# Where the adaLN sums of a decoder layer are kept: two PSUM banks instead of SBUF

## The chip, the cores and the metric

The kernel runs on one core of a Trainium2 chip. The metric is the device time of one execution in microseconds. Besides DMA queues the core has five engines that each work through their own list of instructions in order: TensorE (PE: matmuls and transposes), VectorE (DVE), ScalarE (ACT), GpSimd (POOL) and SyncE (SP, which here issues most of the DMAs). SBUF is the large on-chip memory; PSUM is the small one, of eight banks of 128 partitions x 512 fp32 numbers, that matmuls write.

## The reference, cut to what matters

One decoder layer over 1024 rows of 1024 numbers, in fp32. A conditioning vector c gives six rows of 1024 (shift, scale and gate for each of two sub-layers):

```
cond = silu(c)
mod  = cond @ w_ada + b_ada                       # 1024 x 6144 matrix
sh1, sc1, gt1, sh2, sc2, gt2 = split(mod, 6)
h = rmsnorm(x) * (1 + sc1) + sh1
proj = h @ w_in                                   # q, k, v, indexer q/k/w, conv input
mixed = concat(sparse_attention(...), conformer_conv(...))
x = x + gt1 * (mixed @ w_out)
h = rmsnorm(x) * (1 + sc2) + sh2
x = x + gt2 * (relu(h @ w_up)**2 @ w_down)
out = rmsnorm(x)
```

The change concerns three of the six rows: gt1 (part 2 of the matrix's columns), sh2 (part 3) and sc2 (part 4).

## The kernel before, in words

Every fp32 product is made of three matmuls of rounded halves (hi x hi, hi x lo, lo x hi). So each weight tile, loaded from HBM as `wraw`, is split on the chip: ACT writes `whi` (L184), POOL writes `wlo` = wraw - whi (L185, 128x512). Four half tiles of wraw and six of whi and wlo go round.

The stages in order of time are: an opening (loads of x, first norm, sh1 and sc1, key/value projection), the projection of the indexer's queries (L137), the GLU input of the convolution (L126), the score chain (PE L616 and L617, ACT L618, DVE L621 and L623), a bit-by-bit search of the top-k threshold (ACT L704, DVE L706 and L707), beside it the convolution of 31 taps on DVE (L665 and L667), the attention, the output projection, and the MLP, which fills PE to the end.

A row of mod is not made by matmul alone. The eight 128-row slices of a part of w_ada (tile `wa`, 128x1024, 512 KB, two buffers) are loaded one after the other. DVE multiplies each by the slice's 128 numbers of cond, one a partition, and adds it to a sum of 128x1024, held as two halves of 512: `TENSOR_SCALAR` for the first slice (L547), `SCALAR_TENSOR_TENSOR` for the other seven (L545). A matmul with ones then sums over partitions. `ada_row` (L550 to L555) does that for gt1 by two matmuls of 128x512 (L554), one after the other through one PSUM bank (`po`), each emptied by DVE (L555). `ada_col` (L557 to L563) does it for sh2 and sc2 by eight matmuls of one column each half (L561), read by DVE (L563). Program order is part 2, `ada_row`, part 3, `ada_col`, part 4, `ada_col`.

In the opening sh1 and sc1 are made in the same way by `ada` (L357 to L366), but there the running sum lies in the PSUM bank `cv`, and only the last add writes to SBUF. The convolution (`conv_chunk`, L658 to L668) keeps its running sum in `cv` as well.

The PSUM tiles here are `mm` (two banks), `mc` (two), `tp` (two), `cv` (one) and `po` (one). A tile of a name with one bank can be written only when every reader of the tile before it, in program order, is done. `po` serves in turn the opening's sums over partitions, `ada_row`, `ada_col`, and then the attention's outputs (L772); `cv` serves the opening's `ada` and then the convolution's chunks.

Which instruction comes when on an engine is fixed at build time by a planner: every piece of work carries a number (`tc.cur_priority`, from the table PR), and among what its model of time holds to be ready the lowest number goes first. The evacuation of PSUM is at 30050, weight feed 32050, ada parts 130000 and up, key preparation (L481 to L499) 150500 and up, scores 200000 and up, GLU 205500, the first half's convolution 998450 (last of all). At run time the order stands: an instruction that waits holds back all behind it on its engine or queue, SP's DMA issues too.

Of the kernel before, what the change touches and what calls it, by code (L numbers as in the profile page):

```python
# [9 lines left out]
FT = mybir.dt.float32  # L10
# [5 lines left out]
OP = mybir.AluOpType  # L16
# [3 lines left out]
KD = D // 128  # L20
# [52 lines left out]
def layer(ctx, tc, x, c, positions, w_ada, b_ada, g_mix, w_in, conv_w, conv_b,  # L73
          conv_norm_g, conv_norm_b, w_out, g_mlp, w_up, w_down, g_final, out, dump=None):
    nc = tc.nc
    V, A, P, T, SP = nc.vector, nc.scalar, nc.gpsimd, nc.tensor, nc.sync
# [19 lines left out]
    psum = ctx.enter_context(tc.tile_pool(name="psum", bufs=1, space=bass.MemoryType.PSUM))  # L96
# [7 lines left out]
    def cv_tile(n=512):  # L104
        return psum.tile([128, n], FT, name="cv", bufs=1)
# [98 lines left out]
    cond = const.tile([128, 8], FT, name="cond")  # L204
# [34 lines left out]
    with tc.tile_pool(name="start", bufs=1, reuse_waits="tile") as st:  # L239
# [115 lines left out]
        accs = {}  # L355
# [180 lines left out]
    def ada_part(part):  # L536
        tc.cur_priority = PR["ada"] + 100 * part
        accs = [adacc[:, 2 * (part % 2) + s, :] for s in range(2)]
        for k in range(KD):
            wa = at.tile([128, D], FT, name="wa", tag="sb", bufs=2)  # L540
            SP.dma_start(wa, w_ada[k * 128:(k + 1) * 128, part * D:(part + 1) * D])
            for s in range(2):
                w = wa[:, s * 512:(s + 1) * 512]
                if k:
                    V.scalar_tensor_tensor(accs[s], w, cond[:, k:k + 1], accs[s], op0=OP.mult, op1=OP.add)  # L545
                else:
                    V.tensor_scalar(accs[s], w, cond[:, 0:1], None, op0=OP.mult)  # L547
        return accs

    def ada_row(part, dst, accs):  # L550
# [6 lines left out]
    def ada_col(part, dst):  # L557
        accs = ada_part(part)
        ps = psum.tile([128, 8], FT, name="po")
        for k in range(KD):  # L560
            T.matmul(ps[:, k:k + 1], accs[k // 4][:, (k % 4) * 128:(k % 4 + 1) * 128], ones[:, 0:1],  # L561
                     start=True, stop=True)
        V.tensor_tensor(dst, ps, bada[:, part * 8:part * 8 + 8], op=OP.add)  # L563

    sh2, a2 = modT[:, 16:24], modT[:, 24:32]
    gt1 = at.tile([128, D], FT, name="gt1")
    ada_row(2, gt1, ada_part(2))
    ada_col(3, sh2)
    ada_col(4, a2)
# [719 lines left out]
```

## Time and profile before

| | us |
|---|---|
| median of three runs | 1352.66 (1352.29 to 1352.8) |
| the profiled execution | 1357.23 |
| its span | 1355.5 |

| engine | busy us in the span | share | instructions |
|---|---|---|---|
| PE | 1251.4 | 92% | 6622 |
| DVE | 964.6 | 71% | 2068 |
| ACT | 692.6 | 51% | 1384 |
| POOL | 464.4 | 34% | 386 |

The times below are read from one profiled execution, counted from the start of its span. Its own time is the span and 1.7 us around it. "Busy" is time in which an instruction of the engine runs; a wait is idle time, and is put down to what ended it.

### The profile page before, as it was taken

To read this page: it belongs to the slowest core of one execution; us is meant where nothing else is said; L and a number is where in the kernel's file an instruction comes from. 1 tells how busy PE (TensorE), PEld (TensorE's weight loads), DVE (VectorE), ACT (ScalarE), POOL (GpSimd) and SP (SyncE) were. 2 spreads that over 40 slices of the span, in tenths; PEclk is the share of its full clock that TensorE was granted. 3 is DMA by queue.
4 is the path that set the end of the run, shared out by engine and by line. 5 is a ranking of instruction groups with operands and counts; after the bars stand their busy time and mean duration, and the time that the engine had idled before them with its cause. 6 is when DMAs were issued, how large, how long until landed. Compare 5 with 4: busy or idle time off the path is not lost.

```text
span 1355.5 us, 19285 instructions
## 1 busy us (share of the span) xinstructions
PE 1251.4 (92%) x6622; PEld 1050.2 (77%) x6622; DVE 964.6 (71%) x2068; ACT 692.6 (51%) x1384; POOL 464.4 (34%) x386
## 2 busy tenths in 40 slices
PE   2777899999998999989999999799999999999997
PEld 2676799878987788768887889678878877888875
DVE  6879798988898999988779871662443485444357
ACT  6533377666756988648996643333112232333332
POOL 1132434422144254432133127222212244444453
PEclk9888899999999999989999999899999999999999
DMA  9457634521223132221112122361111243323322
GB/s 314 148 171 231 181 98 129 140 71 56 86 87 125 47 101 87 80 73 59 47 55 71 55 94 90 124 208 54 47 39 47 62 143 121 104 91 101 93 94 93
DMA packets 135690, 139.55 MB, mean 103 GB/s; under 512 B 8877, under 2 KB 109833, under 8 KB 135592
## 3 DMA queue, kind: packets, MB, share of 16 engines
q1 hardware_dynamic: 135424, 138.22, 33.1%
q8 instruction: 52, 0.85, 0.3%
q14 instruction: 46, 0.38, 0.1%
q10 hardware_dynamic: 168, 0.11, 0.0%
HBM read 126.23 MB, written 12.06 MB: 102 GB/s over the span
## 4 chain that ended last, share of the span: by engine, by line
PE 66%; DVE 20%; DMA 4%; ACT 4%; issue 3%; POOL 1%; ACTq 0%; POOLq 0%; SPq 0%; DVEq 0%
PE mm L126 25%; PE mc L126 14%; PE tp L126 7%; PE mm L137 5%; DMA wa<-in_w_ada_dram 3%; DVE cv L667 2%; PE po L865 2%; PE tp L858 2%; DVE acc L545 1%; ACT sj L704 1%; PE po L772 1%; DVE acc L1042 1%; PE mc L846 1%; PE mc L847 1%; DVE e L682 1%
## 5 line engine op out<-in xcount | busy, mean ns | idle before, releaser
L185 POOL TENSOR_TENSOR wlo<-wraw,whi 128x512 fp32r<-128x512 f32 x310 | 413.1, 1341 | 773.3 <-ACT whi L184 682.1
L184 ACT ACTIVATE whi<-wraw 128x512 fp32r<-128x512 f32 x310 | 193.5, 629 | 297.9 <-PE mm L126 142.5
L126 PE MATMUL mm<-half,whi 128*128 128x512 f32 x608 | 204.8, 405 | 0.1
L667 DVE SCALAR_TENSOR_TENSOR cv<-glu,cwT,cv 128x512 f32<-128x512 f32 x232 | 174.0, 750 | 0.7
L704 ACT ACTIVATE sj<-score,bits 128x512 uint8<-128x512 f32 (+5 forms) x186 | 163.3, 878 | 17.1 <-DVE bits L707 8.3
L126 PE MATMUL mc<-half,whi 128*128 128x512 f32 x416 | 150.4, 393 | 0.5 <-ACT half L981 0.5
L126 PE MATMUL mm<-whi,uh 128*128 128x512 f32 x344 | 138.5, 403 | 7.1 <-DVE acc L1042 3.2
L126 PE MATMUL mm<-whi,ul 128*128 128x512 f32 x344 | 137.4, 399 | 3.3 <-DVE ul L1010 3.3
L126 PE MATMUL mm<-wlo,uh 128*128 128x512 f32 x344 | 136.8, 398 | 0.0
L1042 DVE TENSOR_TENSOR acc<-mm,acc 128x512 f32<-128x512 f32 x152 | 104.5, 688 | 44.4 <-PE mm L126 43.1
L1008 DVE TENSOR_TENSOR sq<-sq 128x512 f32<-128x512 f32 x42 | 46.0, 1096 | 126.2 <-ACT sq L1007 126.2
L126 PE MATMUL mc<-half,wlo 128*128 128x512 f32 x336 | 132.1, 393 | 0.0
L126 PEld LDWEIGHTS mm<-half,whi 128*128 128x128 f32 x608 | 115.3, 193 | 20.2 <-ACT half L981 0.3
L126 PE MATMUL mm<-half,wlo 128*128 128x512 f32 x304 | 124.4, 409 | 0.0
L137 PE MATMUL mm<-whi,half 128*128 128x256 f32 x640 | 120.1, 284 | 3.5 <-DVE wi L474 2.8
L137 PEld LDWEIGHTS mm<-whi,half 128*128 128x128 f32 x640 | 101.4, 191 | 5.5 <-issue 2.9
L126 PE MATMUL mc<-h,whi 128*128 128x512 f32 x256 | 100.2, 391 | 0.0
L126 PEld LDWEIGHTS mc<-half,whi 128*128 128x128 f32 x416 | 79.0, 190 | 17.3 <-ACT half L981 0.8
L137 PE MATMUL mm<-wlo,half 128*128 128x256 f32 x320 | 90.6, 283 | 0.4 <-POOL wlo L185 0.4
L126 PEld LDWEIGHTS mm<-whi,uh 128*128 128x128 f32 x344 | 65.3, 190 | 26.1 <-DVE acc L1042 6.5
L126 PEld LDWEIGHTS mm<-whi,ul 128*128 128x128 f32 x344 | 65.3, 190 | 18.1 <-DVE ul L1010 4.2
L126 PEld LDWEIGHTS mm<-wlo,uh 128*128 128x128 f32 x344 | 65.2, 190 | 13.0
(314 smaller groups left out, 2619.2 us busy)
## 6 DMA issues: line engine op xcount, KB each, us to landing
wraw<-in_w_up_dram SPq DMA_DIRECT2D x108, 256.0 KB, 2.8
wraw<-in_w_down_dram SPq DMA_DIRECT2D x108, 256.0 KB, 2.8
wa<-in_w_ada_dram SPq DMA_DIRECT2D x48, 512.0 KB, 4.9
wraw<-in_w_in_dram SPq DMA_DIRECT2D x33, 256.0 KB, 2.8
wraw<-in_w_in_dram SPq DMA_DIRECT2D x64, 128.0 KB, 3.0
wraw<-in_w_out_dram SPq DMA_DIRECT2D x32, 256.0 KB, 2.6
xs<-in_x_dram SPq DMA_DIRECT2D x8, 512.0 KB, 8.1
x<-in_x_dram SPq DMA_DIRECT2D x8, 512.0 KB, 5.1
```

The costliest lines, as they stand in the source:

```text
L126: T.matmul(ps, x, y, start=first and i == 0, stop=last and i == 3 * n - 1)
L137: T.matmul(ps[:, i * 256:(i + 1) * 256], rows[i][k][x], w[k][y], start=m == 0, stop=m == len(steps) - 1)
L184: A.activation(hi, raw, AF.Copy)
L185: P.tensor_tensor(lo, raw, hi.bitcast(FT), op=OP.subtract)
L545: V.scalar_tensor_tensor(accs[s], w, cond[:, k:k + 1], accs[s], op0=OP.mult, op1=OP.add)
L667: V.scalar_tensor_tensor(y if tap == CK - 1 else s, gl[:, tap:tap + 512], cwT[:, j, tap:tap + 1], s, op0=OP.mult, op1=OP.add)
L682: V.tensor_scalar(jk, score[b], thr, 0.0, op0=op, op1=OP.add, accum_out=dst[:, b:b + 1])
L704: A.activation(sj[:, :L], score[b], AF.Sign, bias=bits[:, col].bitcast(FT), accum_out=cnt[:, col])
L858: T.transpose(t[:, 2 * i + u, :], sbp[u][:, (i0 + i) * 128:(i0 + i + 1) * 128], ident)
L865: T.matmul(po[:, hp % 2], vhl[:, i0 + i, g].rearrange("p a d -> p (a d)"), p[:, 2 * i:2 * i + 2, :], start=i0 + i + j == 0, stop=i0 + i == ...
L1008: V.tensor_tensor(sq, sq, sq, op=OP.mult)
L1042: V.tensor_tensor(acc[b][:, cols], ps, acc[b][:, cols], op=OP.add)
```

## The change

In `ada_part`, which makes parts 2, 3 and 4, the running sum of the first half of the columns is kept in a `cv` tile and that of the second half in a new `po` tile. The multiplication of the first slice writes there, slices 1 to 6 read and write there, and slice 7 reads there and writes the finished sum into the SBUF tile `adacc`, from which the matmuls with ones read as before. The loads, the number and shapes of instructions, and the other parts (0 and 1 in the opening, 5 in the MLP) stay.

```diff
     def ada_part(part):
         tc.cur_priority = PR["ada"] + 100 * part
         accs = [adacc[:, 2 * (part % 2) + s, :] for s in range(2)]
+        sums = [cv_tile(), psum.tile([128, 512], FT, name="po")]
         for k in range(KD):
             wa = at.tile([128, D], FT, name="wa", tag="sb", bufs=2)
             SP.dma_start(wa, w_ada[k * 128:(k + 1) * 128, part * D:(part + 1) * D])
             for s in range(2):
                 w = wa[:, s * 512:(s + 1) * 512]
                 if k:
-                    V.scalar_tensor_tensor(accs[s], w, cond[:, k:k + 1], accs[s], op0=OP.mult, op1=OP.add)
+                    V.scalar_tensor_tensor(accs[s] if k == KD - 1 else sums[s], w, cond[:, k:k + 1], sums[s],
+                                           op0=OP.mult, op1=OP.add)
                 else:
-                    V.tensor_scalar(accs[s], w, cond[:, 0:1], None, op0=OP.mult)
+                    V.tensor_scalar(sums[s], w, cond[:, 0:1], None, op0=OP.mult)
         return accs
```

## Rows read from the trace of the kernel before

**Rows 1.** The profile's page: busy time, share of the span, instructions.
```profile
PE 1251.4 (92%) x6622; PEld 1050.2 (77%) x6622; DVE 964.6 (71%) x2068; ACT 692.6 (51%) x1384; POOL 464.4 (34%) x386
```

**Rows 2.** By stretch: busy us of PE, PEld, DVE, ACT, POOL; PEclk, DMA share, GB/s.
```profile
93.00:107.00 14.00, 13.02 (x106) 12.52 (x106) 13.69 (x33) 5.61 (x15) 8.45 (x6) 1.00 0.63 181
107.00:119.00 12.00, 4.43 (x17) 2.70 (x16) 11.11 (x35) 3.39 (x7) 1.27 (x1) 0.61 0.85 235
...
163.00:180.00 17.00, 17.00 (x66) 13.59 (x66) 14.05 (x26) 7.19 (x13) 5.81 (x7) 0.87 0.23 62
```

**Rows 3.** Who waited for whom, 55 to 170 us: total us, times, longest.
```profile
DVE acc L545 <- DMA wa<-in_w_ada_dram: 10.3, 7, 3.9
...
PE po L554 <- DVE gt L555: 7.6, 1, 7.6
```

**Rows 4.** DVE's groups by shape, 75 to 163 us: busy us, mean ns.
```profile
L545 DVE SCALAR_TENSOR_TENSOR acc<-wa,cond,acc 128x512 f32<-128x512 f32 x42 | 36.5, 907 | 10.5 <-DMA wa<-in_w_ada_dram 10.3
...
L547 DVE TENSOR_SCALAR acc<-wa,cond 128x512 f32<-128x512 f32 x6 | 2.6, 480 | 0.0
...
L667 DVE SCALAR_TENSOR_TENSOR cv<-glu,cwT,cv 128x512 f32<-128x512 f32 x2 | 1.5, 744 | 0.0
```

**Rows 5.** Instructions on tiles acc and cv: ns minimum/median/maximum, first and last start.
```profile
L545 DVE SCALAR_TENSOR_TENSOR acc<-wa,cond,acc x42: 739/747/1787, 76.8 to 157.3; 128x512 f32<-128x512 f32 x42
...
L667 DVE SCALAR_TENSOR_TENSOR cv<-glu,cwT,cv x232: 703/749/757, 146.9 to 552.1; 128x512 f32<-128x512 f32 x116
...
L366 DVE TENSOR_SCALAR cv<-wa,cond x4: 747/750/754, 19.2 to 50.4; 128x512 f32<-128x512 f32 x4
```

**Rows 6.** DVE in order of time: start, us, instruction, idle before.
```profile
101.20 2.45 DVE L545 SCALAR_TENSOR_TENSOR acc<-wa,cond,acc 128x512 f32<-128x512 f32 x2
103.57 1.26 DVE L484 TENSOR_TENSOR kk<-ra,rb 128x16 f32<-128x16 f32 x1
...
107.22 0.88 DVE L547 TENSOR_SCALAR acc<-wa,cond 128x512 f32<-128x512 f32 x2
...
110.17 0.18 DVE L481 TENSOR_TENSOR ra<-kk,cs 128x32 f32<-128x32 f32 x1
...
112.25 2.42 DVE L545 SCALAR_TENSOR_TENSOR acc<-wa,cond,acc 128x512 f32<-128x512 f32 x2
114.59 0.68 DVE L555 TENSOR_TENSOR gt<-po,gt 128x512 f32<-128x512 f32 x1
...
117.43 0.69 DVE L555 TENSOR_TENSOR gt<-po,gt 128x512 f32<-128x512 f32 x1 [0.64 <-PE po L554]
```

**Rows 7.** PE in order of time.
```profile
105.56 1.02 PE L554 MATMUL po<-acc,ones 128*128 128x512 f32 x2
...
115.32 2.08 PE L554 MATMUL po<-acc,ones 128*128 128x512 f32 x2 [7.57 <-DVE gt L555]
```

**Rows 8.** POOL in order of time.
```profile
101.49 3.31 POOL L185 TENSOR_TENSOR wlo<-wraw,whi 128x512 fp32r<-128x512 f32 x2 [2.32 <-ACT whi L184]
...
121.54 1.30 POOL L185 TENSOR_TENSOR wlo<-wraw,whi 128x512 fp32r<-128x512 f32 x1 [7.42 <-ACT whi L184]
```

**Rows 9.** SP's queue in order of time.
```profile
108.12 0.33 SPq L541 DMA_DIRECT2D wa<-in_w_ada_dram  x1
108.51 0.43 SPq L179 DMA_DIRECT2D wraw<-in_w_in_dram  x1
```

**Rows 10.** DVE in order of time, later.
```profile
133.42 0.87 DVE L547 TENSOR_SCALAR acc<-wa,cond 128x512 f32<-128x512 f32 x2
...
162.35 0.17 DVE L563 TENSOR_TENSOR modT<-po,vT 128x8 f32<-128x8 f32 x1 [3.80 <-PE po L561]
```

**Rows 11.** PE busy in the matmuls of L126 alone, by stretch.
```profile
107.00:121.50 14.50, 3.89 (x9) 0.65 0.86 251
121.50:126.40 4.90, 4.77 (x17) 1.00 0.68 200
```

**Rows 12.** Who PE waited for, 163 to 280 us.
```profile
PE tp L524 <- DVE qs L519: 4.4, 1, 4.4
```

## The prediction

> **What bounds the kernel now.** I read the page's busy times first, then the busy time by stretch around the changed lines, then who waited for whom, then the engines in order of time. PE is busy for 92% of the span [rows 1], so the 104 us in which it idles are what can be won, and an edit on DVE pays where DVE holds PE up. The changed additions lie between 76.8 and 157.3 us [rows 5]. The reader is to see in [rows 2] that one stretch there is poor: from 107 to 119 us PE works 4.43 of 12 us, at a mean clock of 0.61, while DVE works 11.11 of 12; before it PE works 13.02 of 14, and from 163 to 180 all 17. [rows 3] names the cause: one wait of 7.6 us of the second L554 matmul for the `po` bank, which DVE empties in L555. The first L554 ran at 105.56 [rows 7]; its L555 came only at 114.59 [rows 6], because DVE was late and had other work in front. So in this stretch PE is bound by DVE's order of instructions, and DVE in part by w_ada's loads (10.3 us in seven waits [rows 3]).
>
> **The additions that change place.** L545 takes 747 ns in the median but 1787 at most [rows 5], and 907 in the mean [rows 4]. The same instruction with its sum in PSUM (L667: one input in SBUF, one in `cv`) takes 749 in the median and 757 at most, in 232 cases [rows 5]. So PSUM as such gives nothing (747 against 749); what can go is the tail. Its cause shows at 101.20: a pair that takes 2.45 us, where two medians make 1.49, lies on POOL's wlo work of 101.49 to 104.80 [rows 6, 8]. If all 42 lose their tail, that is 42 x (907 - 747) = 6.7 us of DVE time. The last slice's six still write SBUF, but read one input there, as L667's do. POOL's work goes on, though, and DVE's key preparation between the additions has the same trouble: L484 at 103.57 takes 1.26 us beside the same POOL work, where L481, of twice the size, takes 0.18 without it [rows 6]. A delay that an addition no longer meets can hit the next small instruction. The bounds are therefore 0 (all passed on) and 6.7 us; I take 4.5, nearer to the upper, since POOL's instruction is partly over by the time the next small one comes.
>
> The Trainium skill, "SBUF — State Buffer", section "Who interferes with whom", says that a VectorE instruction with two SBUF inputs contends with a GpSimd instruction that reads SBUF, and one with at most one such input, outside the 2-port modes, doesn't. The rows of L667 agree with the second half. The same section counts two-input tensor_tensor instructions among those that contend, which is what speaks against this change: the key preparation stays exposed. Taken alone, that rule would put the passed-on share near all and the DVE gain near 0; the POOL row at 101.49, which covers both an addition and an L484, is why I don't go so far.
>
> **The first multiplications.** Six L547 take 480 ns from SBUF to SBUF [rows 4]; the same instruction into `cv` in the opening takes 750 [rows 5]. That costs 6 x 0.27 = 1.6 us of DVE. Net on DVE: 4.5 - 1.6 = 2.9 us saved, with bounds -1.6 and +5.1.
>
> **The bank `cv`.** It is free since the opening. But the convolution's first chunk, which now starts on it during part 4 (first tap at 146.9 [rows 5], two taps by 163 us [rows 4]), must wait until part 4 is done, near 157. That moves two taps and the first multiplication, some 3 x 0.75 = 2.2 us, behind 157. DVE then stands idle for 3.80 us until L563 at 162.35 [rows 10], so there is room. The cost is between 0 (all in that gap) and 2.2 us on DVE, if the planned order puts them behind L563; I take 0.5.
>
> **The bank `po`, and the order it enforces.** Now the second half's first multiplication of part 3 has to come behind both L555 of part 2. Today all of part 3's first two slices and the pair at 112.25 stand ahead of the first L555: from 107.22 (0.88 us) to 112.25 (2.42 us) three pairs, 0.88 + 1.41 (an estimate: two medians less their overlap) + 2.42 = 4.7 us [rows 6]. Of these only first-half instructions can stay in front, and with two buffers of `wa` at most two of them: 0.75 + 0.75 = 1.5. So DVE reaches the first L555 about 3.2 us earlier by order, and another 1 us earlier at least by the tail of the 101.20 pair: near 110.4 instead of 114.59. If the key preparation of later positions is moved up into the hole, half of the 3.2 may be lost. PE's wait of 7.6 us shrinks to some 3.4, with bounds 1 and 7.6. At the shortened wait I expect less of the clock loss too: after the present one the two matmuls take 2.08 us where the first pair took 1.02 [rows 7].
>
> In part 4 the same rule puts L547 behind L563 of part 3; L547 came at 133.42 [rows 10], which is already behind that L563 in DVE's order, so nothing moves. PE's L554 and L561 wait for the sums to leave `po`, which is the same last addition for which they wait already: no cost.
>
> **What is late next.** A slot of `wa` is released by both halves of a slice. Part 3's third slice is loaded at 108.12 [rows 9]; with the first slice's second half behind the second L555 (117.43 now, some 113 then) that load goes to about 114. SP issues in order, and 0.4 us behind it stands a load for w_in [rows 9]. If the planned order keeps that sequence, the GLU's weights are late by about 5 us. Is there room? The fourth weight tile of the chunk is split at 121.54 [rows 8]. By 121.5 PE had done 9 of the chunk's 48 L126 (8 row blocks x 3 products x 2 column groups in the code) and by 126.4 it had done 26 [rows 11]; the second half of the weights is first needed with the 25th, near 126. So PE could run some 4 to 5 us earlier before it met the weights as they come now; that caps the gain. The planner, whose model also sees the `wa` load waiting, may put the w_in load in front.
>
> **The sum.** PE wait 7.6 - 3.4 = 4.2 us, and with it up to 1 us of clock, capped by the weights at 4 to 5; I take 4. The DVE saving of 2.9 less 0.5 is partly the same gain (it makes the L555 early) and is not added. From 163 to 180 PE is full [rows 2], so work that starts earlier ends earlier; the search behind it is a chain from the last score, and PE waits again for DVE behind that search (4.4 us [rows 12]), so the shift goes through instead of being swallowed. Sum: 1357.23 - 4 = 1353.2 in terms of the profiled execution. That execution is 4.57 us (0.34%) above the median of the runs; I carry the difference over: 1352.66 - 4 = 1348.7.
>
> **Rivals.**
> 1. *The gain is swallowed.* DVE's delays are passed on to the key preparation (net -1.6 us on DVE), other ready work fills the hole in front of L555, and the chain of w_ada loads still sets the pace: 10.3 us in seven waits [rows 3] speak for it. Then PE's wait stays near 7, and the time stays within 1352.66 +- 2.7, say 1352. Against it: instructions that stood ahead of L555 can't stand there any more.
> 2. *The `po` bank makes it slower.* The planned order fills the hole with key preparation, so that L555 stays at 114.59 and 117.43. Then part 3's first slice ends only near 119, the load of 108.12 goes out some 10 us later, and the w_in load behind it on SP too. The tile split at 121.54 would come near 131.5, against a need near 126: PE waits 5.5 us there, and has won nothing at L555: 1352.66 + 5.5 = 1358.2. The point from which this decides is a second L555 later than about 113 + 2, with SP's order as it is. For it: SP's present order; against it: the planner places loads by when it thinks their slots come free.
> 3. *More is won.* The whole 7.6 us and the clock loss of 2 us go, and the earlier chain of w_ada loads brings the weights earlier by half of the 6.7 us: some 8 us, 1344.7. Against it stands the cap by the weights.
> 4. *A new planned order behind 163 us.* The planner sees new release times, and its choices further on (convolution against search and scores, all on DVE) can fall otherwise, by some microseconds either way; I price it at +- 3 us, an estimate from DVE waits of PE such as that of 4.4 us [rows 12], and hold it in the width of the cases.
>
> **How the numbers follow.** A change of this kernel can be told from none from about 0.2%, 2.7 us. Forecast (1345.5 to 1350): 0.40. Swallowed: 0.27. Slower through the bank or a worse order: 0.26. More won: 0.07. So faster 0.47, same 0.27, slower 0.26. The range of 8 in 10 leaves out the far ends on both sides: 1343.5 to 1358; the likeliest case's own is 1345.5 to 1350.
>
> **What would show it.** Right: L545's longest falls to about 0.76 us while L481 to L499 keep cases above 1 us; the L547 take 0.75; the wait of PE at L554 falls to 2 to 5 us and the stretch of 107 to 119 us shows more than 6 us of PE at a higher clock; the score chain and the search start some 4 us earlier. Wrong: PE's wait at L554 stays at 7 us or turns into one for weights (POOL's wlo or a w_in load) before 135 us; the convolution's first chunk holds PE at the convolution's transposes; or the shift is there at 180 us and gone by 480 us, because a search or a score chain was ordered worse.

## The result and the profile after

The changed kernel takes 1366.24 us in the median of four runs (1364.97 to 1367.66), the kernel before 1352.73 (1352.29 to 1355.49): a ratio of 1.0096, 95% interval [1.0074, 1.0117]. It is slower by 1%. I had forecast 1348.7 us, faster by 0.3%; the result lies outside the range as well. The profiled execution took 1367.66 us, its span 1365.9. In what follows the changed kernel's lines stand one or two higher than before: L546 are the additions (L545 before), L549 the first multiplications (L547), L556 and L557 the gate's matmul and its evacuation (L554, L555), and from there on two are added.

The page's busy times of the changed kernel, which answer to [rows 1]:

```profile
PE 1253.1 (92%) x6622; PEld 1051.1 (77%) x6622; DVE 970.4 (71%) x2068; ACT 696.2 (51%) x1384; POOL 462.4 (34%) x386
```

The number of instructions is the same. PE is busy 1.7 us longer and idle 8.7 us longer in a span that is 10.4 us longer. First the stage that was changed. By tile, in the changed kernel (minimum, median and maximum ns, first and last start), as in [rows 5]:

```profile
L546 DVE SCALAR_TENSOR_TENSOR cv<-wa,cond,cv x18: 744/755/756, 76.6 to 162.7; 128x512 f32<-128x512 f32 x18
L549 DVE TENSOR_SCALAR cv<-wa,cond x3: 744/747/751, 75.1 to 142.9; 128x512 f32<-128x512 f32 x3
L546 DVE SCALAR_TENSOR_TENSOR acc<-wa,cond,cv x3: 733/735/747, 101.3 to 165.6; 128x512 f32<-128x512 f32 x3
L546 DVE SCALAR_TENSOR_TENSOR po<-wa,cond,po x18: 743/750/752, 77.3 to 163.4; 128x512 f32<-128x512 f32 x18
```

The additions' tail, 1787 ns at most before, is gone: none takes over 0.76 us. The multiplications cost 0.75 as foretold. DVE in order of time in the changed kernel shows where the tail went, as in [rows 6]:

```profile
95.46 1.28 DVE L498 CAST nh<-kk 128x256 fp32r<-128x256 f32 x1
...
109.23 1.25 DVE L484 TENSOR_TENSOR kk<-ra,rb 128x16 f32<-128x16 f32 x1
110.51 1.21 DVE L481 TENSOR_TENSOR ra<-kk,cs 128x32 f32<-128x32 f32 x1
111.64 1.30 DVE L481 TENSOR_TENSOR rb<-kk,sn 128x32 f32<-128x32 f32 x1
112.97 1.17 DVE L483 TENSOR_TENSOR kk<-ra,rb 128x16 f32<-128x16 f32 x1
114.07 0.17 DVE L484 TENSOR_TENSOR kk<-ra,rb 128x16 f32<-128x16 f32 x1
114.15 0.68 DVE L557 TENSOR_TENSOR gt<-po,gt 128x512 f32<-128x512 f32 x1
...
117.00 0.69 DVE L557 TENSOR_TENSOR gt<-po,gt 128x512 f32<-128x512 f32 x1 [1.09 <-PE po L556]
...
117.93 0.75 DVE L549 TENSOR_SCALAR po<-wa,cond 128x512 f32<-128x512 f32 x1
```

POOL in the same stretch, in the kernel before and then in the changed one:

```profile
112.84 1.27 POOL L185 TENSOR_TENSOR wlo<-wraw,whi 128x512 fp32r<-128x512 f32 x1 [8.04 <-ACT whi L184]
```

```profile
109.18 4.93 POOL L185 TENSOR_TENSOR wlo<-wraw,whi 128x512 fp32r<-128x512 f32 x4 [3.75 <-ACT whi L184]
```

Key preparation filled the room in front of the first L557 because it took over the delays: beside POOL's run of 109.18 to 114.11 four small instructions need 1.17 to 1.30 us each, where the next one, as POOL ends, needs 0.17. Key preparation itself is hardly more than before: between part 2's last addition and this evacuation stand 31 small instructions of key preparation (on the tiles kk, ra and rb) where 27 stood, about 0.7 us more. But POOL, which split one weight tile there, now splits four in a row, and that makes some 4.2 us (an estimate: 4.93 us for four that need 0.7 undelayed). So L557 came at 114.15 where it was 114.59 before; without these delays it would have come near 110. The first L556 ran 1.5 us earlier than in [rows 7], and PE's wait for `po` grew from 7.57 to 8.95. PE in order of time, then who DVE waited for from 55 to 170 us, as in [rows 3]:

```profile
104.05 1.02 PE L556 MATMUL po<-acc,ones 128*128 128x512 f32 x2
114.88 2.07 PE L556 MATMUL po<-acc,ones 128*128 128x512 f32 x2 [8.95 <-DVE gt L557]
```

```profile
DVE cv L546 <- DMA wa<-in_w_ada_dram: 16.4, 10, 5.1
```

And DVE waits 16.4 us for `wa` where it waited 10.3. The second half's first multiplication of part 3 stands at 117.93, behind the second L557; until then its slice's buffer is held and no new slice can be loaded. SP's queue of the changed kernel:

```profile
102.75 0.33 SPq L542 DMA_DIRECT2D wa<-in_w_ada_dram  x1
103.12 3.52 SPq L179 DMA_DIRECT2D wraw<-in_w_in_dram  x7
110.47 2.10 SPq L179 DMA_DIRECT2D wraw<-in_w_in_dram  x4
118.71 1.32 SPq L542 DMA_DIRECT2D wa<-in_w_ada_dram  x2
```

For 16 us no slice is loaded (the load of 108.12 [rows 9] is that of 118.71). The loads for w_in stand ahead of it now, and PE waits for weights nowhere from 104 to 180 us. Part 4's last addition starts at 166.22 instead of 157.3.

Yet the time isn't lost at once. Same events before and after, each row first of the kernel before, then of the changed kernel (rows by tile; first and last start at the end of each): the search's first sign count, the last evacuation of the attention's scores, the last evacuation of a gate.

```profile
L704 ACT ACTIVATE sj<-score,bits x186: 599/888/1164, 180.6 to 724.0; 128x512 uint8<-128x512 f32 x31, 128x384 uint8<-128x384 f32 x31, 128x1024 uint8<-128x1024 f32 x31, 128x896 uint8<-128x896 f32 x31
...
L848 DVE CUSTOM_DVE_ANT_0 sb<-mc,score x32: 673/688/692, 615.7 to 785.9; 128x512 f32<-128x512 f32 x32
...
L555 DVE TENSOR_TENSOR gt<-po,gt x4: 678/692/693, 114.6 to 994.5; 128x512 f32<-128x512 f32 x4
```

```profile
L706 ACT ACTIVATE sj<-score,bits x186: 600/878/1155, 174.8 to 730.6; 128x512 uint8<-128x512 f32 x31, 128x384 uint8<-128x384 f32 x31, 128x1024 uint8<-128x1024 f32 x31, 128x896 uint8<-128x896 f32 x31
...
L850 DVE CUSTOM_DVE_ANT_0 sb<-mc,score x32: 669/692/693, 619.8 to 801.0; 128x512 f32<-128x512 f32 x32
...
L557 DVE TENSOR_TENSOR gt<-po,gt x4: 679/692/693, 114.2 to 1006.9; 128x512 f32<-128x512 f32 x4
```

The search starts 5.8 us earlier, as forecast or better. At 800 us the kernel is 15.1 us late, at 1000 us 12.4, at the end 10.4 (the spans). What lies between shows by stretch (PE busy and its instructions first, then the other engines; granted clock, DMA share and GB/s last), before and after:

```profile
270.00:430.00 160.00, 152.95 (x1044) 136.54 (x1044) 142.91 (x306) 100.50 (x226) 48.74 (x47) 0.99 0.26 81
...
440.00:460.00 20.00, 19.78 (x93) 15.48 (x94) 18.51 (x44) 19.19 (x36) 3.57 (x3) 0.90 0.09 26
460.00:480.00 20.00, 18.64 (x80) 13.88 (x79) 18.84 (x48) 19.05 (x39) 7.12 (x6) 1.00 0.25 79
```

```profile
270.00:430.00 160.00, 152.96 (x1011) 134.15 (x1010) 143.29 (x297) 97.72 (x218) 45.21 (x43) 0.99 0.23 74
...
440.00:460.00 20.00, 18.16 (x78) 14.24 (x78) 17.42 (x44) 17.51 (x32) 1.91 (x2) 0.74 0.18 55
460.00:480.00 20.00, 15.06 (x60) 10.67 (x59) 19.40 (x52) 19.32 (x41) 5.83 (x5) 0.85 0.22 67
```

From 270 to 430 us the same busy time holds 33 instructions fewer. From 440 to 480 PE idles 6.8 us instead of 1.6, at 0.74 and 0.85 of its clock. At the middle of that place PE, in order of time, before and after:

```profile
465.24 0.39 PE L126 MATMUL mm<-whi,uh 128*128 128x512 f32 x1
```

```profile
475.68 0.79 PE L618 MATMUL mc<-keys,qT 128*128 128x512 f32 x1 [1.91 <-DVE score L625]
...
477.38 0.79 PE L126 MATMUL mm<-whi,uh 128*128 128x512 f32 x1 [0.15 <-ACT uh L1006]
477.97 0.63 PE L126 MATMUL mm<-wlo,uh 128*128 128x512 f32 x1
```

PE's first down product of the MLP starts 12 us later. In PE's order score products (L618) now stand in front of it; they wait for buffers that DVE empties (L625) between ten taps of the convolution, and behind the waits the clock is at the lower of its levels (1.2 GHz: granted 0.50 from 476 to 482 us; the matmuls of 512 columns take 0.63 us, 0.39 before). None of these instructions touches the sums that the change moved. Either the change's local delay (its banks) comes out so late, or the planner, which plans all instructions anew when one dependence changes, has drawn a worse order.

### The profile page after: what moved, and what is told of

It is laid out like the page before. It is cut to its first block, busy times and chain, and to the rows that moved or that the text cites. A ratio compares the mean times of both kernels' runs of the same rounds, so it can differ in the third digit from the quotient of the medians.

```text
span 1365.9 us, 19296 instructions
## 1 busy us (share of the span) xinstructions
PE 1253.1 (92%) x6622; PEld 1051.1 (77%) x6622; DVE 970.4 (71%) x2068; ACT 696.2 (51%) x1384; POOL 462.4 (34%) x386
## 4 chain that ended last, share of the span: by engine, by line
PE 59%; DVE 11%; ACT 2%; issue 2%; POOL 1%; DMA 1%; POOLq 0%; DVEq 0%; ACTq 0%; SPq 0%
PE mm L126 24%; PE mc L126 14%; PE tp L126 7%; PE mm L137 4%; PE po L867 2%; PE tp L860 2%; PE mc L848 1%; PE mc L849 1%; DVE acc L1044 1%; DVE g2acc L1196 1%; DMA wa<-in_w_ada_dram 1%; DVE e L684 1%; PE mc L618 1%; DVE score L625 1%; PE po L774 1%
## 5 line engine op out<-in xcount | busy, mean ns | idle before, releaser
L126 PE MATMUL mm<-half,whi 128*128 128x512 f32 x608 | 205.6, 405 | 1.0 <-ACT half L983 0.6
L126 PE MATMUL mc<-half,whi 128*128 128x512 f32 x416 | 149.0, 390 | 0.5 <-ACT half L983 0.5
L126 PE MATMUL mm<-whi,uh 128*128 128x512 f32 x344 | 139.8, 407 | 3.3 <-DVE acc L1044 1.8
L126 PE MATMUL mm<-whi,ul 128*128 128x512 f32 x344 | 138.3, 402 | 2.2 <-DVE ul L1012 2.2
L126 PE MATMUL mm<-wlo,uh 128*128 128x512 f32 x344 | 138.6, 403 | 0.0
L126 PEld LDWEIGHTS mm<-half,whi 128*128 128x128 f32 x608 | 115.0, 192 | 21.6 <-DVE acc L1044 1.1
L126 PE MATMUL mc<-half,wlo 128*128 128x512 f32 x336 | 131.1, 390 | 0.0
L126 PE MATMUL mm<-half,wlo 128*128 128x512 f32 x304 | 122.7, 403 | 0.0
L126 PE MATMUL mc<-h,whi 128*128 128x512 f32 x256 | 99.9, 390 | 0.0
L126 PEld LDWEIGHTS mc<-half,whi 128*128 128x128 f32 x416 | 78.0, 188 | 17.0 <-ACT half L983 0.8
L126 PEld LDWEIGHTS mm<-whi,uh 128*128 128x128 f32 x344 | 66.2, 192 | 21.1 <-DVE acc L1044 4.4
L126 PEld LDWEIGHTS mm<-whi,ul 128*128 128x128 f32 x344 | 66.0, 192 | 17.7 <-DVE ul L1012 3.3
L126 PEld LDWEIGHTS mm<-wlo,uh 128*128 128x128 f32 x344 | 66.3, 193 | 13.6
```

The source lines that it names most:

```text
L126: T.matmul(ps, x, y, start=first and i == 0, stop=last and i == 3 * n - 1)
```

## The experiments

Three theories. **A**: the bank `cv` is the loss, since the convolution starts behind part 4. **B**: the bank `po` is, since part 3 waits for the gate. **C**: the loss is the new planned order as such. Where the expectations speak of D, that is A and B together: what the change itself does.

**One part of the change at a time.** In `ada_part`, one edit for each kernel:

```diff
 e1   sums = [cv_tile(), accs[1]]
 e2   sums = [accs[0], psum.tile([128, 512], FT, name="po")]
 e3   sums = [cv_tile(), psum.tile([128, 512], FT, name="po")] if part == 2 else accs
 e4   held = [cv_tile(), psum.tile([128, 512], FT, name="po")]
      # sums in SBUF as before; one column of held is written in slice 0 and read in slice 7
```

> Only the first half's sum is in PSUM (bank cv); the second half's stays in SBUF. Three theories for the 13.5 us by which the change made the kernel slower. A, the bank cv: parts 2 to 4 hold it until some 166 us, so the convolution of the first half starts at 170 instead of 142 us, is ten taps behind at 260 us, and its norm comes late: this kernel is then as slow as the whole change, 1362 to 1368. B, the bank po: parts 3 and 4 have to wait for the gate's two evacuations, their sums end 9 us late: this kernel is free of that and takes 1346 to 1353. C, the planned order: any change of what the planner sees here re-plans everything behind it, and the time moves by up to 10 us either way with no respect to which bank it was: anything from 1343 to 1370, with convolution start and ada end as in A and B but no link between them and the time.

Measured: 1354.34 us, ratio 1.0004 [0.9984, 1.0024].

> Only the second half's sum is in PSUM (bank po); the first half's stays in SBUF. A (cv held): the convolution can start near 142 us again, 1346 to 1353. B (po held): as slow as the whole change, 1362 to 1368. C (planned order): anything from 1343 to 1370.

Measured: 1368.26 us, ratio 1.0119 [1.0087, 1.0151].

> Both banks for part 2 alone; parts 3 and 4 sum in SBUF. No bank is held past the gate's own use of it. A and B: no loss, and the tail of part 2's additions is gone: 1346 to 1352. C (planned order): anything from 1343 to 1370; above 1358 speaks against both A and B.

Measured: 1371.0 us, ratio 1.0132 [1.01, 1.0165].

> The sums stay in SBUF as before; one column of a cv tile and of a po tile is written at each part's first slice and read at its last (added times zero), so that the banks are held as in the change, by 12 instructions of one column more. A or B: as slow as the change or slower, 1364 to 1372, since the tails of the additions stay. C (planned order): anything from 1345 to 1375.

Measured: 1369.38 us, ratio 1.0123 [1.0087, 1.016].

A falls with e1, and with e2, whose convolution takes its first tap at 149.5 us (146.9 in the kernel before) and which is slow. e4 speaks against the sums in PSUM as such: its sums are in SBUF, and it is as slow as the change. e3 can't be explained by B: it holds no bank behind the gate, its last sum in a bank is done at 105 us, and it is the slowest of the four. C was left, and a guess about its form: in the order of ACT, 84 or 85 sign counts stood ahead of the first `uh` (the rounded half that the MLP's first down product needs) in the kernel before and e1, and 90 in all the slow ones.

**The guess tested.** e5 and e6 change one number of the planner's table, in the changed kernel and in the kernel before; e7 takes the first `uh` off ACT:

```diff
 e5, e6   PR = {..., 'ada': 206000, ...}        # 130000
 e7       if not first: first.append(1); V.tensor_tensor(uh, sq, sq, op=OP.mult)
          else: A.activation(uh, sq, AF.Square)
```

> The whole change with one number changed: the urgency that the planner gives to the adaLN pieces (ada) is 206000 in place of 130000; all sums are in the two PSUM banks as in the change, and no arithmetic differs. In the order that is planned, ScalarE has 84 sign counts ahead of the first rounded half of the MLP (uh), where the changed kernel, e2, e3 and e4 have 90 and the kernel before and e1 have 85 and 84. Theory C (the loss is the new planned order, and the place of that first uh behind the sign counts near 465 us is the greater part of it): fast, 1346 to 1357 us, TensorE above 17.5 us busy at a clock above 0.95 in 460 to 480 us, first uh near 463 us. Theory D (what the change itself does costs the time, through the banks, the reads of PSUM, or the dependences between the parts): as the change, 1362 to 1370 us, with 460 to 480 us near 15 us busy.

Measured: 1380.66 us, ratio 1.0197 [1.0161, 1.0232].

> The kernel before, its sums in SBUF, with the same one number changed (ada 206000 in place of 130000): nothing of the change is in it. In its planned order 90 sign counts stand ahead of the first uh. Theory C: slow, 1362 to 1372 us, first uh on ScalarE at 473 us or later, TensorE at 14.5 to 16 us busy in 460 to 480 us at a clock below 0.9. Theory D: as the kernel before, 1351 to 1356 us.

Measured: 1365.45 us, ratio 1.0091 [1.0061, 1.0121].

> The whole change, with one instruction moved: the first uh of the MLP's first half is a square on VectorE (sq times sq, rounded on output) in place of one on ScalarE, so that TensorE's first down product doesn't stand behind ScalarE's sign counts. Everything else is as in the change, but the order is planned again. The uh of the second unit stays on ScalarE and still has 90 sign counts ahead of it. Theory C in its narrow form (the wait for the first uh itself is the loss): TensorE's 460 to 480 us recovers to above 17 us busy and the time falls by 5 to 9 us against the change, to 1357 to 1361 us. Theory C in its wide form (the whole order around 440 to 480 us and behind is what matters, and the first uh is only its mark): the second unit's uh is late next, and the time stays within 4 us of the change, 1362 to 1370 us. Theory D: as the change, 1366 us.

Measured: 1366.69 us, ratio 1.0098 [1.0066, 1.0129].

e6 is the first proof that an order alone can cost 0.9%: nothing in it is changed but one number of the table. (It isn't the changed kernel's order: the gate's first evacuation comes at 139.1 us there.) But the guess about its form fell twice: e5 has its 84 and is the slowest kernel of all, and e7 wins nothing. In e7 the score products hold PE as before, and behind them stands a wait for DVE (PE, in order of time):

```profile
475.63 0.79 PE L618 MATMUL mc<-keys,qT 128*128 128x512 f32 x1 [1.66 <-DVE score L625]
...
479.73 0.80 PE L126 MATMUL mm<-whi,ul 128*128 128x512 f32 x1 [1.30 <-DVE ul L1017]
```

The late `uh` was a mark of the order, not the cause.

**The order held.** Now each instruction got as its priority its place in an order to be kept, so that the planner has little left to choose:

```diff
+        def call(*a, **k):
+            self.tc.cur_priority = self.left[0]      # the place in the order that is to be kept
+            self.left = self.left[1:]
+            r = f(*a, **k)
```

How near a kernel comes to the order that it was to keep stands in its expectation. In these kernels all instructions are issued from one line, shown as L96.

> The kernel of e3 (the PSUM sums for part 2 alone, ratio 1.0132), whose instructions are the same, but with the order of the kernel before: every instruction's priority in the planner is its place in the order of the kernel before. That comes out almost to the letter: 23 of 6474 TensorE instructions, 30 of 2050 on VectorE and 10 of 1099 on ScalarE stand out of the old sequence, all near part 2's own stretch, where e3 had 914, 668 and 273. Theory C (the loss is the new order behind the stage, not one wait at the first uh): as the kernel before or up to 4 us faster, 1348 to 1357 us. Theory D (the change's own sums, banks or dependences cost it): as e3, 1366 to 1372 us.

Measured: 1348.22 us, ratio 0.9951 [0.9932, 0.9971].

> The kernel before, its sums in SBUF, with the changed kernel's order as priorities: 42 of 6474 TensorE instructions and 66 of 1099 on ScalarE stand out of the changed kernel's sequence (405 of 2050 on VectorE, most of them by few places). Nothing of the change's arithmetic or banks is in it. Theory C: slow, 1362 to 1374 us (the changed kernel's loss, and the additions' waits of the kernel before with it), TensorE near 15 us busy in 460 to 480 us. Theory D: as the kernel before, 1351 to 1357 us.

Measured: 1369.8 us, ratio 1.0112 [1.0079, 1.0145].

> The whole change with the order of the kernel before as priorities. The two banks don't allow all of it: 470 of 6474 TensorE instructions stand out of the old sequence (826 in the changed kernel). Theory C: between, nearer to the kernel before, 1346 to 1362 us, and which of the slow stretches it has can be read from its profile. Theory D: as the change, 1362 to 1370 us.

Measured: 1355.06 us, ratio 1.0017 [0.9994, 1.004].

> The whole change with the order of e1 (the first half's sums alone in a bank, ratio 1.0004) as priorities: 268 of 6474 TensorE instructions stand out of e1's sequence. Theory C: near e1, 1346 to 1360 us, and the place where a version that beats both kernels could be found. Theory D: as the change, 1362 to 1370 us.

Measured: 1358.89 us, ratio 1.0041 [1.0019, 1.0064].

e8 and e9 settle C. The instructions of e3, slow by 1.3%, are fast by 0.5% in the old order; the old instructions are slow by 1.1% in the new one. The place about 460 us goes with the order and not with the sums (by stretch, e8 and then e9, columns as above):

```profile
440.00:460.00 20.00, 20.00 (x100) 16.12 (x98) 18.50 (x47) 19.36 (x38) 6.44 (x5) 1.00 0.20 57
460.00:480.00 20.00, 18.61 (x80) 13.94 (x79) 18.88 (x46) 19.04 (x39) 8.31 (x7) 1.00 0.23 71
```

```profile
440.00:460.00 20.00, 15.19 (x64) 11.51 (x65) 18.53 (x45) 17.43 (x35) 3.81 (x4) 0.74 0.28 97
460.00:480.00 20.00, 15.64 (x75) 11.90 (x73) 19.24 (x54) 19.71 (x40) 7.74 (x6) 1.00 0.26 79
```

The whole change in the old order (e10) and in that of e1 (e11) lies near the kernel before, 0.2% and 0.4% above it, and not where the change in its own order lies; theory D falls with that as the whole explanation. Left open were the stretch in which the order costs, and why the whole change in the old order (e10) doesn't gain what part 2 alone does.

**Where the order costs.** The two orders were spliced on the kernel before, at a given time:

```diff
 e12   priorities: the changed kernel's order up to 270 us, then that of the kernel before
 e13   that of the kernel before up to 270 us, then the changed kernel's
 e14   that of the kernel before up to 430 us, then the changed kernel's
```

> The kernel before, its sums in SBUF. Priorities: up to 270 us (1334 TensorE instructions) the changed kernel's order, behind that the order of the kernel before. Against the kernel before 262 of 6474 TensorE instructions are out of sequence, nearly all in the first part; against the changed kernel 720. Theory C1 (the loss sits in the order behind 270 us, above all about 440 to 480 us and 800 us; what the additions' stage does to the order before 270 us is only its trigger): near the kernel before, 1349 to 1359 us, TensorE above 18 us busy in 460 to 480 us. Theory C2 (the loss sits in the order before 270 us, such as the convolution's taps that are put behind the search, and all later order only bears it): as e9, 1362 to 1372 us.

Measured: 1360.36 us, ratio 1.0047 [1.0027, 1.0066].

> The counterpart: the kernel before, up to 270 us (1337 TensorE instructions) in its own order, behind that in the changed kernel's order. 226 of 6474 TensorE instructions are out of the changed kernel's sequence and 661 out of that of the kernel before. C1: slow, 1361 to 1372 us, TensorE near 15 us busy in 440 to 460 or 460 to 480 us. C2: as the kernel before, 1350 to 1358 us.

Measured: 1367.84 us, ratio 1.0073 [1.0047, 1.01].

> The kernel before, up to 430 us (2381 TensorE instructions) in its own order, behind that in the changed kernel's order: 390 of 6474 TensorE instructions are out of the sequence of the kernel before. C1 with the loss about 440 to 480 us and behind: slow, 1358 to 1370 us. C1 with the loss between 270 and 430 us, or C2: as the kernel before, 1350 to 1358 us. With e13 this says on which side of 430 us the loss lies.

Measured: 1357.08 us, ratio 1.0015 [0.9995, 1.0035].

Neither C1 nor C2 holds alone, and the loss has two places: the order before 270 us costs some 0.5%, that behind 270 us some 0.7%, and behind 430 us alone it can't be told from nothing. So about 460 us is where the loss is seen, and before 430 us is where most of it is made. By stretch, e13 and e14:

```profile
270.00:430.00 160.00, 152.24 (x1014) 135.10 (x1015) 144.65 (x306) 98.23 (x219) 45.09 (x43) 0.98 0.24 76
...
460.00:480.00 20.00, 14.82 (x59) 10.81 (x58) 19.42 (x53) 18.79 (x38) 5.30 (x5) 0.85 0.22 66
```

```profile
270.00:430.00 160.00, 153.53 (x1045) 136.81 (x1045) 142.90 (x305) 99.88 (x225) 51.17 (x49) 0.99 0.26 83
...
460.00:480.00 20.00, 15.60 (x54) 11.50 (x52) 19.70 (x53) 19.14 (x38) 5.80 (x5) 0.74 0.14 44
```

e13, in the old order to 270 us, does 1014 PE instructions from there to 430 us like the changed kernel (1011); e14 does 1045 like the kernel before (1044). e14 too has a poor stretch at 460 to 480 us, and its total is hardly worse: a poor stretch alone doesn't show what a kernel loses. The spliced orders are followed only in the main (in e14 390 of PE's 6474 instructions are out of the old sequence), so the two shares are rough.

**What the whole change loses in the old order.** Which sums lie in which bank, with the order of the kernel before as priorities (`po` stands for a tile of that bank):

```diff
 e15   sums = [cv_tile(), po if part == 2 else accs[1]]
 e16   sums = [cv_tile(), po if part != 3 else accs[1]]
 e17   sums = [cv_tile() if part == 2 else accs[0], po if part != 4 else accs[1]]
```

> Both banks for part 2, for parts 3 and 4 the first half's bank alone, and the order of the kernel before as priorities (445 of 6474 TensorE instructions out of the old sequence, 23 in e8). It asks what of the whole change takes e8's gain of 0.5% away in e10 (ratio 1.0017). If the second half's bank at parts 3 and 4 takes it (theory B: the gate's product waits for that bank): as e8 or faster, 1344 to 1351 us. If the first half's bank takes it (theory A: the convolution starts behind part 4's sums): as e10, 1351 to 1358 us. If it is the order that a held bank still shifts, whatever the bank: 1350 to 1360 us too, and the profiles must tell A from it by where the taps start.

Measured: 1349.86 us, ratio 0.9948 [0.9929, 0.9968].

> The whole change but for one place: the second half's sums of part 3 stay in SBUF (no po bank for part 3); part 2 and part 4 have both banks, part 3 the first half's. Order of the kernel before as priorities (449 of 6474 TensorE instructions out of the old sequence). If part 3's po bank takes the gain (the gate's product has the same po buffers, and its gated weights wait for part 3's last additions): as e15, ratio 0.993 to 0.998, 1344 to 1352 us, and TensorE's wait for the gated weights gt near 4 us as in e15 (8.1 in e10). If part 4's po bank takes it: as e10, ratio 1.000 to 1.004, 1353 to 1359 us.

Measured: 1346.24 us, ratio 0.9944 [0.9923, 0.9964]. It beats both kernels, by 0.56% and 1.5%.

> The opposite: part 2 has both banks, part 3 the po bank alone, part 4 none (nothing in the convolution's bank behind part 2). Order of the kernel before as priorities (460 of 6474 TensorE instructions out of the old sequence). If part 3's po bank takes the gain: the wait for gt at 7 to 9 us and the ratio 0.999 to 1.005, 1351 to 1360 us. If not: as e8, ratio 0.993 to 0.997, 1344 to 1351 us.

Measured: 1357.1 us, ratio 1.0031 [1.0012, 1.005].

In the old order it is the bank `po` at part 3 and no other: the kernels without it gain (e8, e15 and e16: 0.9944 to 0.9951), those with it don't (e10 and e17: 1.0017 and 1.0031), though all but e8 are about equally far from the old order (445 to 470 PE instructions). So theory B comes back beside C, in the form that this bank at part 3, with the order that the planner makes around it, costs 0.7%. The two aren't separated: by the traces (PE's instructions by tile, in order of their start) at least 298 of e10's 6622 stand out of e16's sequence and 242 of e17's, where e15 and e16 differ by 9. What PE waited for from 90 to 440 us, first e16, then e10:

```profile
PE tp L96 <- DVE qs L96: 6.2, 3, 5.6
...
PE po L96 <- DVE gt L96: 2.6, 1, 2.6
```

```profile
PE po L96 <- DVE gt L96: 8.1, 1, 8.1
PE mm L96 <- ACT glu L96: 5.2, 1, 5.2
```

The gate's wait is 2.6 us without the bank at part 3 (4.0 in e15) and 8.1 with it. But e8 waits 6.7 and e17 6.6, of which the one gains and the other doesn't, so this wait isn't the whole of it; I had expected 7 to 9 for e17. Another difference is the chain of slices. The last additions of part 4 (by tile), in e16 and in e10:

```profile
L96 DVE SCALAR_TENSOR_TENSOR acc<-wa,cond,po x2: 740/742/743, 103.4 to 155.0; 128x512 f32<-128x512 f32 x2
```

```profile
L96 DVE SCALAR_TENSOR_TENSOR acc<-wa,cond,po x3: 735/740/743, 102.7 to 165.1; 128x512 f32<-128x512 f32 x3
```

They start at 155.0, 155.3 and 155.7 us in e16, e15 and e8, and at 165.1, 166.9 and 166.2 in e10, e17 and the changed kernel. The convolution's first chunk ends behind that (last tap at 189.9 us in e16, 193.3 in e15, 199.1 in e10, 198.9 in e17), and e10 and e17 have a wait of PE for `glu` of 5.2 and 4.4 us between 260 and 340 us, which e16 hasn't. That the late chunk causes that wait fits the traces, but no run isolates it, and e16 waits about as long there for `qs` (5.6 us at 270.7). A second candidate is the search: its first sign count, in e16 and then in e10 (by tile):

```profile
L96 ACT ACTIVATE sj<-score,bits x186: 598/886/1162, 175.1 to 717.8; 128x512 uint8<-128x512 f32 x31, 128x384 uint8<-128x384 f32 x31, 128x1024 uint8<-128x1024 f32 x31, 128x896 uint8<-128x896 f32 x31
```

```profile
L96 ACT ACTIVATE sj<-score,bits x186: 599/886/1160, 182.4 to 723.2; 128x512 uint8<-128x512 f32 x31, 128x384 uint8<-128x384 f32 x31, 128x1024 uint8<-128x1024 f32 x31, 128x896 uint8<-128x896 f32 x31
```

It starts 7.3 us later in e10, and 9.1 in e17 (184.2), before any wait for `glu`; at the end they are 7.1 and 11.0 us behind e16 (the spans). But the changed kernel, with the same bank at part 3, starts its search at 174.8 in its own order. By which way the bank at part 3 costs its 0.7% stays open.

## Why the prediction was wrong

**The step that failed.** It is the price of the fourth rival, "a new planned order behind 163 us": ± 3 us, held in the width of the cases. In ratios the whole change comes apart like this: 1.0096 in its own order, 1.0017 in the old one (e10), 0.9944 without part 3's second bank (e16). So the order costs 0.8%, 10.7 us of 1354; the bank at part 3, with what it changes in the order, 0.7%, 9.9 us; and the rest of the change gains 0.56%, 7.6 us (each of these to some 0.3%, by the intervals). The shares depend on the kernel that they are taken from: for part 2 alone the order's share is 1.8%, 24.5 us (e3 against e8), and on the kernel before one number of the table makes 0.9% (e6). The size of ± 3 came from one wait of 4.4 us; a single wait was the wrong measure for hundreds of instructions that change places. Which way an order falls couldn't be read from the trace; that the old order was a good one is known only now (e6, e9 and e13, all on the kernel before, are all worse). An order far from it needn't be slower, though: some 880 of PE's instructions in e1 stand out of the old sequence by its trace, and its ratio is 1.0004. The width on the slow side should have been 15 us at the least, and for e3 25.

**The additions.** Right in the mechanism, with one term mis-sized. The tail went (1787 to 756 ns at most), the multiplications cost 0.27 us each, and the delays were in part handed on to the key preparation: its 72 instructions take 26.5 us from 70 to 170 us where they took 22.3 (counts times means). So 4.3 of the 6.7 us were handed on, where I took 2.2, and net on DVE some 0.8 us of the forecast 2.9 is left.

The rule of the Trainium skill, "SBUF — State Buffer", section "Who interferes with whom", that a VectorE instruction with two SBUF inputs contends with a GpSimd one that reads SBUF, and one with at most one such input, outside the 2-port modes, doesn't, agrees with this trace on both sides: PSUM sums at most 756 ns, small two-input instructions 1.17 to 1.30 us.

**The first bank.** Right in sign and small: the first tap moved from 146.9 to 171.9 us, much further than the 157 that I had, and e1 shows no loss (1.0004), e15 none either.

**The second bank and the order it enforces.** Wrong. I had L555 near 110.4 and PE's wait at 3.4 us; it came at 114.15, and the wait was 9.0. The text named an exception, key preparation moved up into the hole, and priced it at half of 3.2 us. The hole was filled wholly, but by delay: four instructions more make 0.7 us, and those that POOL's four splits hold up make 4.2. The term that failed is again what is handed on, and I had counted on POOL's work where it stood before, with one split at 112.84. My second rival came true in half: its point of decision (a second L555 later than about 115: it came at 117.00) and the late load (108.12 went to 118.71). Its price didn't: the loads for w_in went in front, PE waited for no weights, and the 5.5 us that it put there don't appear. What the bank at part 3 costs in the old order, 9.9 us, is not that chain. The rival had only 0.26 together with all other ways of being slower. Without part 3's bank the wait for the gate shrinks to 4.0 us in e15, 4.4 in e1 and 2.6 in e16, the size that I had forecast; but it is 6.7 in e8 and 5.8 in e3, which have no bank there either.

**What would show it.** The last sign of wrongness in the prediction, a shift that is there at 180 us and gone by 480, is what happened: 5.8 us ahead at 175 us, 12 us behind at 477. In e8 and e16, where neither the order nor part 3's bank stands against it, a gain is there, 6.6 and 7.6 us, and it goes through as I had said: the search starts 4.9 and 5.5 us earlier than in the kernel before, and the last evacuation of the attention's scores is 5.7 and 5.8 us earlier. That the size is near my 4 us is partly luck: in e8 the wait for the gate went from 7.6 to 6.7 us only, where I had 3.4. From 105 to 180 us PE idles 7.6 us in e8 and 6.1 in e16, 11.6 before; which of the changed instructions brings the rest isn't shown.

## What to carry to other kernels

Where a planner fixes the order at build time, a small edit is two changes: the edit and a new order of everything behind it. Measure them apart, by running the edited instructions in the old order and the old instructions in the new one, before any cause is sought in the edit. And a sum kept in a bank that another step is about to use ties its operand's buffers too: ask what load can't start while the first slice waits for that bank.

## What the hardware showed that I had not expected

A first multiplication, with one SBUF input and its result in SBUF, is delayed beside POOL as well. In e8, DVE and then POOL in order of time:

```profile
133.33 1.43 DVE L96 TENSOR_SCALAR acc<-wa,cond 128x512 f32<-128x512 f32 x1
135.29 0.47 DVE L96 TENSOR_SCALAR acc<-wa,cond 128x512 f32<-128x512 f32 x1
...
133.19 1.30 POOL L96 TENSOR_TENSOR wlo<-wraw,whi 128x512 fp32r<-128x512 f32 x1 [0.87 <-ACT whi L96]
```

The same instruction takes 1.43 us beside POOL and 0.47 without it. With its result in PSUM it takes 0.75 and never more than 751 ns in six cases of the changed kernel, two of which lie on a split of POOL's (103.97 on that of 104.15, 143.5 on that of 143.56): slower, but not delayed there. The cast at 95.46 has one SBUF input as well (1.28 us beside POOL's run of 92.71 to 97.89, and 0.29 at 103.56). The rule of the Trainium skill that is quoted above, "SBUF — State Buffer", section "Who interferes with whom", excepts the 2-port modes; no row here shows in which mode these instructions ran, so whether they are a case of that exception is open.
